# Loading the first tile of a masked softmax as two transfers instead of one

## The chip, the core and the metric

The kernel runs on one core of one Trainium2 chip. The metric is the device time of one execution in microseconds (us); the figure for a kernel is the median of several runs.

## What is computed

For each of 16 batch entries, a softmax over the last axis is taken over the first `length` columns only; the columns behind are zero in the output. The input is 16 x 8 x 256 x 256 float32, and the lengths lie between 128 and 255.

```python
result = np.zeros_like(x)
for b in range(batch):
    length = lengths[b]
    masked = x[b, :, :, :length].copy()
    masked = masked - np.max(masked, axis=-1, keepdims=True)
    exp_masked = np.exp(masked)
    result[b, :, :, :length] = exp_masked / np.sum(exp_masked, axis=-1, keepdims=True)
```

## The kernel before

One batch entry is one tile: 2048 rows of 256 numbers, laid out as 128 partitions x 16 rows x 256 columns, so that one partition holds 16 KB that are contiguous in memory. A tile is 2048 KB. Eight slots of the buffer `xt` hold tiles; a tile is loaded into its slot, worked on in place, and stored from there.

For each tile the engines do the following.

- VectorE (DVE) masks the upper half of the columns (`clip`, line 246): beyond the length the value becomes a very large negative number. For the first tile this is two instructions of eight rows each, for the others one of sixteen.
- ScalarE (ACT) takes the exponential in place: the first four rows in one instruction (line 372), the other twelve one by one with their row sums (line 375).
- DVE sums the first four rows (line 267), then for each half tile takes the reciprocal of the row sums (line 277) and multiplies (line 280).
- SyncE (SP) stores the tile in one to four pieces (line 152), each after the multiplication that it needs. SP also lets a tile's store wait until the stores of the tile two before have landed (line 151).

The loads come from two queues. SP issues the load of the first tile as its first transfer (line 143), and afterwards only stores: the hardware queue, called q1 in the profile, carries this load and all stores. GpSimd (POOL) issues the other fifteen loads on the software queue, q0. Three of them are issued at the start (line 194), after the mask limits are ready and one memset has run; the other twelve follow in a loop (line 166), each after an earlier load has landed and the slot's store is done. For most tiles only the columns up to a rounded length are loaded.

The first tile's load counts up the semaphore `s_ld[0]`, and DVE waits for its full count in `mask(0, ...)` before the first `clip`. A transfer's full count is 16. From there on DVE works through its instructions in a fixed order, and everything that it does later stands behind that first wait. SP's first store, two rows per partition of tile 0, waits for the first multiplication.

After the last tile DVE tests whether the sums were in range, and the program ends when the last store has landed.

Of the kernel before, what the change touches and what calls it, by code (L numbers as in the profile page):

```python
# [21 lines left out]
def kernel(  # L22
# [6 lines left out]
    nc = tc.nc  # L29
# [5 lines left out]
    nt = rows // P  # L35
# [4 lines left out]
    x_f = x.rearrange("b h q k -> b (h q) k").rearrange("b (p t) k -> b p t k", p=P)  # L40
# [9 lines left out]
    def batch_of(pos):  # L50
        return pos + 1 if pos < ahead - 1 else {ahead - 1: 15, 15: 0}.get(pos, pos)
# [22 lines left out]
    xt = pool.tile([P, slots, nt, seq_k], F32, name="xt")  # L74
# [24 lines left out]
    sem = lambda n: ctx.enter_context(nc.semaphore(n))  # L99
# [6 lines left out]
    with tc.tile_critical(sync_engine=POOL, no_gpsimd_drain=True):  # L106
# [1 line left out]
        s_ones = sem("s_ones")  # L108
        s_lenb = sem("s_lenb")
        s_lenf = sem("s_lenf")  # L110
        s_ld = [sem(f"s_ld{k}") for k in range(2)]

        s_sw = [sem("s_sw0"), sem("s_sw1")]

# [25 lines left out]


        nc.scalar.dma_start(out=word64, in_=lengths[None, :]).then_inc(s_word, 16)
        nc.sync.dma_start(out=xt[:, 0], in_=x_f[batch_of(0)]).then_inc(s_ld[0], 16)
        for b in range(batch):
            s_b = s_st[b % 2] if b < late else s_late if b < batch - 1 else s_last
            for s in parts(b):
# [3 lines left out]
                if 2 <= b < late and s.start == 0:  # L150
                    nc.sync.wait_ge(s_b, 64 * (b // 2 + 2))
                nc.sync.dma_start(
                    out=out_f[batch_of(b), :, s, :], in_=xt[:, b % slots, s, :]
# [67 lines left out]
        def step(ins):  # L221
# [8 lines left out]
                out=down, in0=iota_i, scalar1=0.5, scalar2=-big, op0=ALU.add, op1=ALU.mult  # L230
# [7 lines left out]
                out=len_s, in0=len_f, scalar1=big, scalar2=None, op0=ALU.mult  # L238
# [4 lines left out]
        def clip(b, s, lo, hi):  # L243

            t = xt[:, b % slots, s, lo:hi]
            return nc.vector.scalar_tensor_tensor(  # L246
                out=t,
                in0=down[:, None, lo:hi].to_broadcast([P, s.stop - s.start, hi - lo]),
                scalar=len_s[:, batch_of(b) : batch_of(b) + 1],
                in1=t,  # L250
                op0=ALU.add,
                op1=ALU.min,
            )

        def mask(b, s):
            if b == 0:
                nc.vector.wait_ge(s_ld[0], 16)
            elif b == ahead - 1:
                nc.vector.wait_ge(s_ld[1], 16)
            else:  # L260
                par = (b - 1 if b < ahead else b) % 2
                nc.vector.wait_ge(s_sw[par], 16 * max(b // 2, 1))
            clip(b, s, mid, seq_k).then_inc(s_min, 1)
# [10 lines left out]
        def divide(b, h):  # L274
# [10 lines left out]
            ).then_inc(s_out, 1)  # L285

        mask(0, slice(0, half))
        mask(0, slice(half, nt))
        total(0)
        for b in range(batch):  # L290


            first = b != 1
            if first:
                divide(b, 0)
            if b + 1 < batch:
                mask(b + 1, slice(0, nt))
            if not first:
                divide(b, 0)
            divide(b, 1)  # L300
            if b + 1 < batch:
                total(b + 1)
# [14 lines left out]
        for k, (_, _, edge, op) in enumerate(checks):  # L317
            nc.vector.tensor_scalar(  # L318
                out=bad[:, k : k + 1],
# [13 lines left out]
        with nc.vector.Else():  # L333
            with nc.Fori(0, batch, 1, engines=[DVE]) as i:
                nc.vector.wait_ge(g_ld, 16 * i + 16)
                nc.vector.scalar_tensor_tensor(
                    out=g_t,
# [8 lines left out]
                    out=neg_max, in_=g_t, op=ALU.max, axis=AX, negate=True  # L346
# [5 lines left out]
                    out=g_t,  # L352
# [10 lines left out]
        with nc.Fori(0, batch // slots, 1, engines=[ACT]) as turn:  # L363
            for slot in range(slots):
                for h in range(2):
# [7 lines left out]
                    for j in range(h * half + lump * (1 - h), (h + 1) * half):  # L373
                        e = xt[:, slot, j, :]
                        ins = nc.scalar.activation(  # L375
                            out=e, in_=e, func=EXP, accum_out=row_sum[:, slot, j : j + 1]
# [5 lines left out]
        with nc.scalar.If(a_redo >= 1):  # L382
# [4 lines left out]
            with nc.Fori(0, batch, 1, engines=[ACT]) as i:  # L387
                nc.scalar.dma_start(out=g_t, in_=x_g[:, bass.ds(i, 1)]).then_inc(g_ld, 16)
                nc.scalar.wait_ge(g_v, 3 * i + 2)
                with nc.Fori(0, nt, 1, engines=[ACT]) as t:  # L390
                    e = g_t[:, bass.ds(t, 1), :]
                    nc.scalar.activation(
                        out=e,
                        in_=e,
# [42 lines left out]
```

## Time and profile before

| | |
|---|---|
| median of 3 runs | 154.32 us (154.25 to 154.43) |
| the profiled execution | 154.43 us |
| its span in the trace | 152.8 us |
| DVE busy | 134.7 us |
| ACT busy | 95.0 us |
| bytes moved by the DMA engines | 61.57 MB, mean 403 GB/s |

The span begins with the first instruction in the trace and ends with the last event; what lies between span and time is outside the trace. A row of the timeline gives start and duration in us, the engine (SPq and POOLq are the queues from which SP and POOL issue), the line of the kernel, the operation, and in brackets the idle time before it and what ended it. A row of the windows gives one stretch of the span: busy time of each engine, and at the end the mean busy share of the 16 DMA engines and the rate in GB/s. A transfer over 128 partitions is spread over the 16 DMA engines, and a packet in the trace is one contiguous piece of it. A packet is counted in the stretch in which it starts, so a share can stand above 1.

### The profile page before, as it was taken

To read this page: it belongs to the slowest core of one execution; us is meant where nothing else is said; L and a number is where in the kernel's file an instruction comes from. 1 tells how busy PE (TensorE), PEld (TensorE's weight loads), DVE (VectorE), ACT (ScalarE), POOL (GpSimd) and SP (SyncE) were. 2 spreads that over 40 slices of the span, in tenths; PEclk is the share of its full clock that TensorE was granted. 3 is DMA by queue.
4 is the path that set the end of the run, shared out by engine and by line. 5 is a ranking of instruction groups with operands and counts; after the bars stand their busy time and mean duration, and the time that the engine had idled before them with its cause. 6 is when DMAs were issued, how large, how long until landed. Compare 5 with 4: busy or idle time off the path is not lost.

```text
span 152.8 us, 817 instructions
## 1 busy us (share of the span) xinstructions
PE 0.3 (0%) x2; PEld 0.2 (0%) x2; DVE 134.7 (88%) x107; ACT 95.0 (62%) x402; POOL 21.3 (14%) x29
## 2 busy tenths in 40 slices
PE   0000000000000000000000000000000000000000
PEld 0000000000000000000000000000000000000000
DVE  1058999999999999999999999999999999889920
ACT  3019599808668493939486684939394866829200
POOL 4961110030303020030300303011030000000000
DMA  4999999999999999999999999999999999999993
GB/s 107 425 425 433 422 413 389 444 412 408 406 396 421 402 421 414 415 408 402 428 411 420 415 414 413 418 414 414 419 419 420 416 419 417 425 442 429 431 418 154
DMA packets 10070, 61.57 MB, mean 403 GB/s; under 512 B 834, under 2 KB 946, under 8 KB 6226
## 3 DMA queue, kind: packets, MB, share of 16 engines
q1 hardware_dynamic: 5328, 35.65, 56.7%
q0 software_dynamic: 4736, 25.89, 41.7%
q14 instruction: 4, 0.03, 0.1%
q10 hardware_dynamic: 2, 0.00, 0.0%
HBM read 27.98 MB, written 33.55 MB: 403 GB/s over the span
## 4 chain that ended last, share of the span: by engine, by line
DMA 82%; DVE 8%; issue 3%; POOL 1%; POOLq 1%; PE 0%; ACTq 0%
DMA xt<-in_x_dram 82%; DVE xt L280 5%; DVE xt L246 2%; POOL xt L189 1%; DMA word<-in_lengths_dram 1%; DVE row_sum L267 1%; POOLq L166 1%; DVE ends L315 0%; POOL xt L194 0%; DVE inv_sum L277 0%; DVE bad L318 0%; DVE len_s L237 0%; PE len_f L214 0%; PE count L216 0%; DVE len_b L234 0%
## 5 line engine op out<-in xcount | busy, mean ns | idle before, releaser
L375 ACT ACTIVATE xt<-xt 128x256 f32<-128x256 f32 x192 | 76.6, 400 | 0.0
L280 DVE TENSOR_TENSOR xt<-xt,inv_sum 128x2048 f32<-128x2048 f32 x32 | 73.4, 2292 | 1.1
L372 ACT ACTIVATE xt<-xt 128x1024 f32<-128x1024 f32 x16 | 16.9, 1057 | 45.7 <-DVE xt L246 45.7
L246 DVE SCALAR_TENSOR_TENSOR xt<-down,len_s,xt 128x2048 f32<-128x2048 f32 (+1 forms) x17 | 37.7, 2220 | 7.2 <-DMA xt<-in_x_dram 7.2
L375 ACT ACTIVATION_READ_ACCUMULATOR xt<-xt 128x1 f32 x192 | 35.9, 187 | 0.0
L166 POOL DMA_DIRECT2D xt<-in_x_dram x12 | 13.3, 1106 | 90.5 <-DMA xt<-in_x_dram 72.8
L267 DVE TENSOR_REDUCE row_sum<-xt 128x4 f32<-128x1024 f32 x16 | 19.4, 1212 | 0.0
L277 DVE RECIPROCAL inv_sum<-row_sum 128x8 f32<-128x8 f32 x32 | 6.4, 199 | 0.9 <-ACT xt L375 0.4
L189 POOL MEMSET xt<- 128x1536 f32 x4 | 5.4, 1398 | 1.1 <-DVE len_s L237 1.1
L359 ACT ACT_TABLE_LOAD x1 | 1.3, 1283 | 1.6 <-PEq L421 1.6
L194 POOL DMA_DIRECT2D xt<-in_x_dram x3 | 1.8, 591 | 0.0
L229 DVE TENSOR_SCALAR down<-iota_i 128x256 f32<-128x256 int32 x1 | 0.3, 301 | 1.6 <-POOL iota_i L179 1.6
L315 DVE TENSOR_REDUCE ends<-inv_sum 128x1 f32<-128x256 f32 x2 | 0.7, 408 | 0.0
L237 DVE TENSOR_SCALAR len_s<-len_f 128x16 f32<-128x16 f32 x1 | 0.2, 174 | 0.4 <-PE len_f L214 0.4
L216 PE MATMUL count<-bad,ones_c 128*1 128x3 bf16 x1 | 0.2, 165 | 143.4 <-DVE bad L318 143.4
L234 DVE CAST len_b<-word 1x16 bf16<-1x16 int32 x1 | 0.2, 163 | 0.4 <-DMA word<-in_lengths_dram 0.4
L179 POOL IOTA iota_i<- 128x256 int32 x1 | 0.3, 333 | 0.6 <-POOLq L106 0.6
L326 DVE TENSOR_REDUCE redo<-count 1x1 f32<-1x3 f32 x1 | 0.1, 150 | 0.3 <-PE count L216 0.3
L318 DVE TENSOR_SCALAR bad<-ends 128x1 bf16<-128x1 f32 x3 | 0.3, 150 | 0.0
L185 POOL MEMSET seed<- 1x1 f32 x2 | 0.2, 226 | 0.0
L216 PEld LDWEIGHTS count<-bad,ones_c 128*1 128x1 bf16 x1 | 0.1, 79 | 143.5 <-DVE bad L318 143.5
L359 ACT ACTIVATE warm<-const-float32-0.0 128x1 f32<-128x1 f32 x1 | 0.2, 203 | 0.0
(10 smaller groups left out, 1.1 us busy)
## 6 DMA issues: line engine op xcount, KB each, us to landing
out_dram<-xt SPq DMA_DIRECT2D x23, 1024.0 KB
xt<-in_x_dram POOLq DMA_DIRECT2D x4, 2048.0 KB, 16.5
xt<-in_x_dram POOLq DMA_DIRECT2D x3, 1728.0 KB, 18.2
out_dram<-xt SPq DMA_DIRECT2D x9, 512.0 KB
out_dram<-xt SPq DMA_DIRECT2D x2, 2048.0 KB
xt<-in_x_dram POOLq DMA_DIRECT2D x2, 1600.0 KB, 17.7
xt<-in_x_dram POOLq DMA_DIRECT2D x2, 1280.0 KB, 17.7
xt<-in_x_dram SPq DMA_DIRECT2D x1, 2048.0 KB, 8.2
```

The costliest lines, as they stand in the source:

```text
L166: nc.gpsimd.dma_start(out=xt[:, slot, :, :w], in_=x_n[:, b, :, :w]).then_inc(s_sw[par], 16)
L189: nc.gpsimd.memset(xt[:, b, :, low:], 0.0).then_inc(s_fill, 1)
L194: nc.gpsimd.dma_start(out=xt[:, b], in_=x_f[batch_of(b)]).then_inc(s_sw[b - 1] if b < 3 else s_ld[1], 16)
L216: nc.tensor.matmul(count, lhsT=ones_c, rhs=bad, start=True, stop=True).then_inc(s_count, 1)
L246: return nc.vector.scalar_tensor_tensor(out=t, in0=down[:, None, lo:hi].to_broadcast([P, s.stop - s.start, hi - lo]), scalar=len_s[:, batc ...
L267: nc.vector.tensor_reduce(out=row_sum[:, b % slots, :lump], in_=xt[:, b % slots, :lump, :], op=ALU.add, axis=AX,).then_inc(s_exp[0], 1)
L277: step(nc.vector.reciprocal(out=inv_sum[:, b, s], in_=row_sum[:, b % slots, s]))
L280: nc.vector.tensor_tensor(out=t, in0=t, in1=inv_sum[:, b, s, None].to_broadcast([P, half, seq_k]), op=ALU.mult,).then_inc(s_out, 1)
L315: step(nc.vector.tensor_reduce(out=ends[:, k : k + 1], in_=values, op=op, axis=AX))
L359: nc.scalar.activation(out=warm, in_=nc.const_aps.tensor(0.0, (P, 1), F32), func=EXP)
L372: nc.scalar.activation(out=e, in_=e, func=EXP).then_inc(s_lump, 1)
L375: ins = nc.scalar.activation(out=e, in_=e, func=EXP, accum_out=row_sum[:, slot, j : j + 1])
```

## The change

The first tile is loaded by two transfers from SP, one behind the other on the same queue: rows 0 and 1 of each partition (2 KB per partition, 256 KB in all), then rows 2 to 15 (14 KB per partition, 1792 KB). Each has a semaphore of its own, `s_ld[0]` and the new `s_ld[2]`. Both calls of `mask` for the first tile wait for both semaphores, so no instruction of DVE uses the first two rows before the other fourteen are there. Nothing else differs; the order of the instructions on the other engines is the same.

```diff
-        s_ld = [sem(f"s_ld{k}") for k in range(2)]
+        s_ld = [sem(f"s_ld{k}") for k in range(3)]
...
-        nc.sync.dma_start(out=xt[:, 0], in_=x_f[batch_of(0)]).then_inc(s_ld[0], 16)
+        for k, s in enumerate((slice(0, 2), slice(2, nt))):
+            nc.sync.dma_start(out=xt[:, 0, s], in_=x_f[batch_of(0), :, s]).then_inc(
+                s_ld[2 * k], 16
+            )
...
             if b == 0:
-                nc.vector.wait_ge(s_ld[0], 16)
+                for k in (0, 2):
+                    nc.vector.wait_ge(s_ld[k], 16)
```

## The prediction

> **What bounds the kernel now.** I read the page first: busy times, the slices of the span, the DMA queues and the chain that ended last.
>
> ```profile
> span 152.8 us, 817 instructions
> PE 0.3 (0%) x2; PEld 0.2 (0%) x2; DVE 134.7 (88%) x107; ACT 95.0 (62%) x402; POOL 21.3 (14%) x29
> DMA  4999999999999999999999999999999999999993
> ...
> q1 hardware_dynamic: 5328, 35.65, 56.7%
> q0 software_dynamic: 4736, 25.89, 41.7%
> ...
> DMA 82%; DVE 8%; issue 3%; POOL 1%; POOLq 1%; PE 0%; ACTq 0%
> ```
>
> Two resources are nearly full. The DMA engines show 9 in every slice but the first and the last, and their two queues together fill 56.7 + 41.7 = 98.4% of the span. DVE is busy for 88%. The chain names DMA for 82%. Which of them sets the end must be read at the two ends of the span, because the change lies at the very start. First the timeline, at the start and near the end:
>
> ```profile
> 1.08 0.39 SPq L143 DMA_DIRECT2D xt<-in_x_dram  x1
> 4.36 1.76 POOL L194 DMA_DIRECT2D xt<-in_x_dram  x3
> 9.39 2.48 DVE L246 SCALAR_TENSOR_TENSOR xt<-down,len_s,xt 128x1024 f32<-128x1024 f32 x2 [6.40 <-DMA xt<-in_x_dram]
> 15.84 2.35 DVE L246 SCALAR_TENSOR_TENSOR xt<-down,len_s,xt 128x2048 f32<-128x2048 f32 x1
> 15.95 0.35 SPq L152 DMA_DIRECT2D out_dram<-xt  x1
> ...
> 134.12 2.35 DVE L246 SCALAR_TENSOR_TENSOR xt<-down,len_s,xt 128x2048 f32<-128x2048 f32 x1 [0.81 <-DMA xt<-in_x_dram]
> ...
> 142.75 2.29 DVE L280 TENSOR_TENSOR xt<-xt,inv_sum 128x2048 f32<-128x2048 f32 x1
> ```
>
> The list of waits has no other wait of DVE for a load:
>
> ```profile
> DVE xt L246 <- DMA xt<-in_x_dram: 7.2, 2, 6.4
> ```
>
> DVE waits for tile 0 until 9.39 and then runs without a wait for a load until just before 134.12, where it waits 0.81 us for the last tile to be masked. Its last multiplication starts at 142.75 and ends at 145.04. What the DMA engines have left by then stands in the windows of the last stages:
>
> ```profile
> 144.00:148.00 4.00, 0.17 (x1) 0.08 (x1) 2.20 (x8) 0.00 (x0) 0.00 (x0) 1.00 0.98 414
> 148.00:152.00 4.00, 0.00 (x0) 0.00 (x0) 0.00 (x0) 0.00 (x0) 0.00 (x0) 1.00 0.60 254
> ```
>
> After 145.04 they still move about 2.96 us x 414 GB/s + 4 us x 254 GB/s = 1225 + 1016 = 2241 KB. DVE's last half tile is 1049 KB of that (128 x 2048 x 4 bytes). So 1192 KB of older stores lie ahead of it, 2.9 us at 414 GB/s. The end is therefore set by the DMA engines working off their bytes. DVE could finish its last multiplication up to 2.9 us later before the DMA engines ran dry, and the first 0.81 us of a delay at the start would even be swallowed by the wait at 134.12. That is the main reading: **the time is the start of the first packets, plus all bytes at the DMA engines' rate, plus a tail**, and DVE's own start has slack.
>
> **The change part by part.** The rate of the packets comes from the DMA view, cut to the stretch from 5 to 6 us (tile 0's load alone), then 8 to 9 us (its last completion markers beside POOL's loads), then 20 to 21 us (POOL's loads beside SP's first store, which has 2 KB per partition).
>
> ```profile
> q1 hardware_dynamic: 25, 0.41, 96.2%
> ...
> q0 software_dynamic: 26, 0.43, 99.3%
> q1 hardware_dynamic: 12, 0.02, 4.4%
> ...
> q0 software_dynamic: 20, 0.33, 77.3%
> q1 hardware_dynamic: 21, 0.04, 11.0%
> ```
>
> A 16 KB packet takes 0.962 x 16 engine-us / 25 = 0.616 us. A 2 KB packet takes 0.110 x 16 / 21 = 0.084 us, against an eighth of the large one, 0.077. (The 2 KB packets are stores, the nearest row there is for 2 KB reads.) In the second stretch q1 has one data packet (0.02 MB) and eleven markers: 0.044 x 16 = 0.70 us, less 0.616, leaves 0.008 us per marker.
>
> 1. *Packets.* Before, each of the 16 DMA engines moves 8 packets of 16 KB and one marker: 4.94 us. After, it moves 8 of 2 KB, a marker, 8 of 14 KB (0.539 each) and a marker: 0.67 + 4.31 + 0.02 = 5.00. That is +0.06 us on the path that sets the end. Bounds: 0, if small reads go at the large ones' rate, and +0.13, twice that.
>
> 2. *SP.* One more issue of 0.39 us (row L143). SP's next transfer is the store at 15.95, so SP has over 13 us of cover and this costs nothing itself. What matters is whether the second transfer's packets reach the DMA engines before the first one's run out. They follow by 0.39 us in issue, and the first 256 KB last 0.67 us. If the trip from issue to engine is the same for both, there is no gap: 0.
>
> 3. *The start of the engines.* This is the term that the trace doesn't show for a split load, so it needs bounds. The windows of the first stretches:
>
> ```profile
> 2.00:2.50 0.50, 0.00 (x0) 0.00 (x0) 0.16 (x1) 0.50 (x1) 0.00 (x0) 1.00 1.84 328
> 2.50:3.00 0.50, 0.17 (x1) 0.10 (x1) 0.17 (x1) 0.49 (x2) 0.00 (x0) 1.00 0.18 33
> 3.00:3.50 0.50, 0.00 (x0) 0.00 (x0) 0.00 (x0) 0.14 (x1) 0.46 (x1) 1.00 0.95 262
> 3.50:4.00 0.50, 0.00 (x0) 0.00 (x0) 0.00 (x0) 0.00 (x0) 0.50 (x1) 1.00 0.86 360
> 4.00:4.50 0.50, 0.00 (x0) 0.00 (x0) 0.00 (x0) 0.00 (x0) 0.50 (x2) 1.00 0.93 393
> ```
>
> From 2.0 to 2.5 us ten packets start (328 GB/s x 0.5 us = 164 KB), and they take 1.84 x 0.5 x 16 / 10 = 1.47 us each, more than twice the 0.616 of later ones. One more starts before 3.0, and the others of the 16 engines only after that. From 2.0 to 4.0 the engines start (328 + 33 + 262 + 360) x 0.5 = 492 KB; at the steady 393 they would start 786 KB. So the start-up loses 294 KB, or 0.75 us. With smaller first packets that loss can shrink to nothing (-0.75) or come a second time for the second transfer (+0.75). I take 0: the late engines and the slow first packets look like a wait until data begins to flow, at about 3 us, and the same bytes then flow whichever way they are cut. The nearest row for packets of 2 KB, 0.084 us, shows no cost of a fresh start.
>
> 4. *DVE.* Two waits more, already met when reached. The 32 multiplications of line 280 each stand behind a wait, and idle 1.1 us in all:
>
> ```profile
> L280 DVE TENSOR_TENSOR xt<-xt,inv_sum 128x2048 f32<-128x2048 f32 x32 | 73.4, 2292 | 1.1
> ```
>
> That is 0.034 us each, so 0 to 0.07 us for two, on DVE and under its cover. If the 2.9 us were gone, they would be paid in full.
>
> 5. *Landing of tile 0.* DVE's start moves with the later of the two markers. Terms 1 and 3 put it at +0.06, with ends at -0.75 and +0.8. There is one further effect. POOL's first three loads, issued at 4.36, have their first packets after 7 us (the DMA view from 6 to 7 us, where q1 is alone, and from 7 to 8 us):
>
> ```profile
> q1 hardware_dynamic: 29, 0.48, 111.3%
> ...
> q1 hardware_dynamic: 24, 0.31, 72.9%
> q0 software_dynamic: 5, 0.08, 19.1%
> ```
>
> Tile 0's packets thus go ahead of POOL's in nearly all cases. With 14 KB packets, each engine has more of them outstanding when POOL's arrive. If one POOL packet gets in between, that engine's marker comes 0.62 us later; if two, 1.23. DVE would then start at 10.0 to 10.6 instead of 9.39, POOL's packets just that much earlier. No DMA engine idles for it. SP's stores begin later, but until about 20 us the engines have POOL's loads to do: three tiles of 2097 KB at 414 GB/s alone are 15.2 us from about 8. At the other end DVE's cover is 2.9 us. So this costs nothing; without the cover it would cost 0.6 to 1.2.
>
> Sum: +0.06 (packets) + 0 (SP) + 0 (start-up) + 0 (DVE) + 0 (landing). The profiled run was 154.43 with a span of 152.8, so 1.6 us lie outside the trace and stay. It becomes 154.49; the median of the runs stands 0.11 below the profiled one, and 154.32 + 0.06 gives **154.4 us**. A measurement of this kernel can tell about 0.2%, 0.31 us, from no change, so this is "the same".
>
> **The rivals.**
>
> *A second start-up (slower).* On the engines that start late, the second transfer's packets come after the first's are done, and the start-up loss of 0.75 us is paid again, with all 16 engines idle or slow and no other load in the queue: POOL issues at 4.36 and its packets start after 7. Time: 154.32 + 0.06 + 0.75 = 155.1. For it: the first ten engines start nearly 1 us before the last five, so handing out a transfer seems to take longer than the 0.39 us of its issue, and the second must wait for the first. Against it: the late engines also run their small packets late. It decides from the point where an engine gets its second batch more than 0.67 us after its first. Chance 0.28.
>
> *The two transfers one after the other (slower).* If the second moved only once the first had landed, the trip itself would be paid twice. The load landed 8.2 us after its issue, of which 4.94 are packets, so the trip and the start-up are 3.3.
>
> ```profile
> xt<-in_x_dram SPq DMA_DIRECT2D x1, 2048.0 KB, 8.2
> ```
>
> POOL's packets could fill the engines in the last part, from about 6 us; about 2 us of idle would remain, 156.4. Against it: SP waits for nothing between the two. The Trainium skill's page "DMA: Bandwidth & Descriptors" (Anatomy of one DMA) gives a software-queue DMA a fixed 2.0 us besides its bytes, and its rules for authors want at least 1 MiB per transfer; by that the 256 KB piece would add 2.0 us, if it were paid in sequence. No run here shows two loads in a row on an empty queue. Chance 0.04.
>
> *A shorter start-up (faster).* If the slow first packets are slow because each engine must finish 16 KB before going on, 2 KB pieces get through sooner. Half of the 0.75 us would be won on the engines' path: 154.32 + 0.06 - 0.38 = 154.0; a gain beyond 0.75 is excluded, as no more is lost. Against it: after 4 us the same 16 KB packets run at full rate, so size alone isn't slow. Chance 0.21.
>
> *The split has no use at all.* DVE waits for both parts, so nothing starts earlier on two rows; that is within my forecast.
>
> **How the numbers follow.** My forecast (154.1 to 154.6) has 0.47, the second start-up 0.28, the serial trip 0.04, the shorter start-up 0.21. The range of 153.9 to 155.1 takes in the forecast, most of the faster case and the second start-up up to its full price; it leaves out the serial trip and the far ends, about 0.15. Faster by over 0.2%: 0.21; within: 0.47; slower: 0.32.
>
> **What would show it.** In the profile after: two L144 issues on SP, 0.39 us apart; in the windows from 2.0 to 4.0 us about 492 KB started again (clearly more speaks for the shorter start-up, clearly less for the second); `clip` of tile 0 between 9.2 and 10.6; the wait before the last mask shrinking by whatever DVE starts later; DMA share still near 1 up to 150 us. I am wrong if the end moves with DVE's start although stores are still queued behind its last multiplication, or if the DMA engines idle in the middle of the span.

## The result, and the profile after

The changed kernel takes 154.75 us (median of 22 runs, 154.46 to 156.03), against 154.37 us for the kernel before (22 runs beside it, 154.18 to 154.77). The ratio is 1.0031, with a 95% interval of 1.0020 to 1.0043: slower by about 0.5 us (the two medians lie 0.38 us apart), a little more than the 0.2% that the prediction took as the bound of "the same". In two further measurements it was 1.0031 (1.0019 to 1.0043) and 1.0027 (1.0017 to 1.0037). The profiled execution took 154.76 us, its span is 153.1 us. The runs also scatter more: 1.6 us from the lowest to the highest, against 0.6.

First the timeline after, then its waits:

```profile
1.08 0.86 SPq L144 DMA_DIRECT2D xt<-in_x_dram  x2
4.37 1.76 POOL L197 DMA_DIRECT2D xt<-in_x_dram  x3
9.64 2.48 DVE L249 SCALAR_TENSOR_TENSOR xt<-down,len_s,xt 128x1024 f32<-128x1024 f32 x2 [6.64 <-DMA xt<-in_x_dram]
16.20 0.34 SPq L155 DMA_DIRECT2D out_dram<-xt  x1
...
134.02 2.35 DVE L249 SCALAR_TENSOR_TENSOR xt<-down,len_s,xt 128x2048 f32<-128x2048 f32 x1 [0.47 <-DMA xt<-in_x_dram]
142.64 2.29 DVE L284 TENSOR_TENSOR xt<-xt,inv_sum 128x2048 f32<-128x2048 f32 x1
```

```profile
DVE xt L249 <- DMA xt<-in_x_dram: 7.1, 2, 6.6
```

The first mask starts 0.25 us later (9.64 for 9.39). In this execution the delay isn't seen at the end: the wait for the last tile is 0.47 instead of 0.81, and the last multiplication starts at 142.64, even 0.11 earlier. Yet the span is 0.3 us longer. DVE did not lengthen it.

The DMA engines ran behind. The windows give the rate in the last column; here first the kernel before, then the changed one:

```profile
2.00:4.00 2.00, 0.17 (x1) 0.10 (x1) 0.34 (x2) 1.13 (x2) 0.96 (x1) 1.00 0.96 246
4.00:6.00 2.00, 0.00 (x0) 0.00 (x0) 0.00 (x0) 0.00 (x0) 2.00 (x4) 1.00 0.94 401
6.00:10.00 4.00, 0.00 (x0) 0.00 (x0) 0.61 (x1) 0.00 (x0) 4.00 (x4) 1.00 1.02 434
50.00:144.00 94.00, 0.00 (x0) 0.00 (x0) 92.02 (x68) 64.31 (x275) 8.07 (x7) 1.00 1.02 418
144.00:152.00 8.00, 0.17 (x1) 0.08 (x1) 2.20 (x8) 0.00 (x0) 0.00 (x0) 1.00 0.79 334
```

```profile
2.00:4.00 2.00, 0.17 (x1) 0.10 (x1) 0.34 (x2) 1.12 (x2) 0.95 (x1) 1.00 0.94 267
4.00:6.00 2.00, 0.00 (x0) 0.00 (x0) 0.00 (x0) 0.00 (x0) 2.00 (x4) 1.00 0.93 387
6.00:10.00 4.00, 0.00 (x0) 0.00 (x0) 0.36 (x1) 0.00 (x0) 4.00 (x4) 1.00 0.99 414
50.00:144.00 94.00, 0.00 (x0) 0.00 (x0) 92.36 (x68) 64.29 (x275) 8.04 (x7) 1.00 1.02 418
144.00:152.00 8.00, 0.17 (x1) 0.08 (x1) 2.09 (x8) 0.00 (x0) 0.00 (x0) 1.00 0.81 344
```

Rate times length gives the KB started in each stretch. By 10 us the kernel before has started 492 + 802 + 1736 = 3030 KB, the changed one 534 + 774 + 1656 = 2964: it leads by 42 KB at 4 us and is 66 KB behind at 10. From 50 to 144 us both run at 418 GB/s; over 94 us one GB/s is 94 KB, so this row alone can't tell whether the changed kernel catches up. The last row can: after 144 us 2672 KB are left before (8 x 334), 2752 after. These 80 KB more are, at 418 GB/s, 0.19 us of the 0.33 between the two profiled executions. Packets are counted where they start, so such a figure is uncertain by some tens of KB; the second profile of the kernel before, below, differs by 32.

### The profile page after: what moved, and what is told of

Read it like the earlier page. It is cut to its first block, busy times and chain, and to the rows that moved or that the text cites. A ratio compares the mean times of both kernels' runs of the same rounds, so it can differ in the third digit from the quotient of the medians.

```text
span 153.1 us, 819 instructions
## 1 busy us (share of the span) xinstructions
PE 0.3 (0%) x2; PEld 0.2 (0%) x2; DVE 134.7 (88%) x107; ACT 95.0 (62%) x402; POOL 21.3 (14%) x29
## 3 DMA queue, kind: packets, MB, share of 16 engines
q1 hardware_dynamic: 5472, 35.65, 56.5%
## 4 chain that ended last, share of the span: by engine, by line
DMA 82%; DVE 8%; issue 3%; POOL 1%; POOLq 1%; PE 0%; ACTq 0%
DMA xt<-in_x_dram 81%; DVE xt L284 4%; DVE xt L249 2%; POOL xt L192 1%; DMA word<-in_lengths_dram 1%; DVE row_sum L271 1%; POOLq L169 1%; DVE ends L319 0%; POOL xt L197 0%; DVE inv_sum L281 0%; DVE bad L322 0%; DVE len_s L240 0%; PE len_f L217 0%; PE count L219 0%; DVE len_b L237 0%
```

## The experiments

Each ratio is to the kernel before, run beside it on the same chip.

**What the ratios are worth.** The kernel before as an experiment of its own, unchanged:

> The kernel before once more, as any other kernel: every theory expects a ratio of 1.000. How far it lies from 1 shows what the other ratios are worth, and a second profile shows how far the first 10 us and the stretch from 20 to 28 us scatter by themselves.

Measured: 154.27 us, ratio 1.0000 (0.9991 to 1.0009). Its second profile:

```profile
2.00:4.00 2.00, 0.17 (x1) 0.10 (x1) 0.34 (x2) 1.12 (x2) 0.95 (x1) 1.00 1.03 254
4.00:6.00 2.00, 0.00 (x0) 0.00 (x0) 0.00 (x0) 0.00 (x0) 2.00 (x4) 1.00 0.94 401
6.00:10.00 4.00, 0.00 (x0) 0.00 (x0) 0.60 (x1) 0.00 (x0) 4.00 (x4) 1.00 1.02 438
144.00:152.00 8.00, 0.17 (x1) 0.08 (x1) 1.61 (x8) 0.00 (x0) 0.00 (x0) 1.00 0.78 330
```

By 10 us 508 + 802 + 1752 = 3062 KB, 32 ahead of its first profile, and 2640 left after 144 us, 32 fewer. So a lead at 10 us can be seen again at the end, but both profiled executions took 154.43 us: 32 KB don't show in the time. Nor does the end of DVE's work: here its last multiplication starts 0.59 us earlier than in the first profile (142.16 for 142.75). And the wait for the last tile is 0.21 instead of 0.81 without any change, so a wait some tenths shorter, as in the changed kernel, doesn't by itself show a delay that was swallowed.

```profile
133.53 2.35 DVE L246 SCALAR_TENSOR_TENSOR xt<-down,len_s,xt 128x2048 f32<-128x2048 f32 x1 [0.21 <-DMA xt<-in_x_dram]
...
142.16 2.29 DVE L280 TENSOR_TENSOR xt<-xt,inv_sum 128x2048 f32<-128x2048 f32 x1
```

**The changed kernel twice more**, no edit:

> The changed kernel once more. Theory A (a second start-up: the first large packets after the small ones are slow again, so all DMA engines run some 0.1 to 0.5 us behind, for good): ratio 1.0025 (+0.4 us), the DMA engines behind the kernel before from about 9 us on. Theory B (DVE's later start sets the end): the same ratio, but the DMA engines level with the kernel before until DVE's start, about 9.6 us, and the loss later. Theory C (the two kernels differ only by scatter): ratio within 0.001 of 1.

> The changed kernel a third time: ratio 1.003. If the loss is a start-up of varying length, the rate from 2 to 4 us lies between those of its first two profiles (267 and 135 GB/s) or near one of them, and the time goes with the KB that are missing by 10 us.

Measured: 154.82 us, 1.0031 (1.0019 to 1.0043), and 154.67 us, 1.0027 (1.0017 to 1.0037). Their profiled executions took 155.07 and 154.72 us. The windows of the second profile, then of the third:

```profile
2.00:4.00 2.00, 0.17 (x1) 0.10 (x1) 0.34 (x2) 1.12 (x2) 0.95 (x1) 1.00 0.97 135
4.00:6.00 2.00, 0.00 (x0) 0.00 (x0) 0.00 (x0) 0.00 (x0) 2.00 (x4) 1.00 0.95 397
6.00:10.00 4.00, 0.00 (x0) 0.00 (x0) 0.00 (x0) 0.00 (x0) 4.00 (x4) 1.00 1.02 434
144.00:152.00 8.00, 0.17 (x1) 0.08 (x1) 2.71 (x8) 0.00 (x0) 0.00 (x0) 1.00 0.84 354
```

```profile
2.00:4.00 2.00, 0.17 (x1) 0.10 (x1) 0.34 (x2) 1.12 (x2) 0.95 (x1) 1.00 0.99 246
4.00:6.00 2.00, 0.00 (x0) 0.00 (x0) 0.00 (x0) 0.00 (x0) 2.00 (x4) 1.00 0.89 373
6.00:10.00 4.00, 0.00 (x0) 0.00 (x0) 0.06 (x1) 0.00 (x0) 4.00 (x4) 1.00 0.98 416
144.00:152.00 8.00, 0.17 (x1) 0.08 (x1) 2.12 (x8) 0.00 (x0) 0.00 (x0) 1.00 0.82 348
```

By 10 us they are 230 and 128 KB behind the first profile of the kernel before, and after 144 us 160 and 112 KB more are left than there. With the first profile of the change that makes three executions:

| | behind by 10 us | left over after 144 us | the same at 418 GB/s | longer than the first profiled execution before |
|---|---|---|---|---|
| first | 66 KB | 80 KB | 0.19 us | 0.33 us |
| second | 230 KB | 160 KB | 0.38 us | 0.64 us |
| third | 128 KB | 112 KB | 0.27 us | 0.29 us |

Each is behind by 10 us, and by how much differs from one execution to the next. That fits the wider scatter of this kernel's runs. The deficit at 10 us and the one at the end have the same sign, not the same size, and the time doesn't simply go with the KB missing by 10 us, as was expected of the third: 62 KB more are missing there than in the first, and it took 0.04 us less. The rest of the time, 0.02 to 0.26 us, isn't resolved by these counts. Nor is the stretch in which the KB go missing always the same: from 2 to 4, 4 to 6 and 6 to 10 us the first execution gains 42, loses 28 and loses 80 KB, the second loses 222, 8 and 0, the third 0, 56 and 72.

Which packets are slow is seen in the DMA view from 2 to 3 us and from 3 to 4 us, here of the first, the second and the third profile:

```profile
q1 hardware_dynamic: 112, 0.22, 65.1%
...
q1 hardware_dynamic: 51, 0.32, 123.2%
```

```profile
q1 hardware_dynamic: 93, 0.19, 151.1%
...
q1 hardware_dynamic: 24, 0.08, 43.8%
```

```profile
q1 hardware_dynamic: 98, 0.19, 78.3%
...
q1 hardware_dynamic: 60, 0.30, 120.0%
```

In the second profile the 93 packets of 2 KB that start from 2 to 3 us take 1.511 x 16 / 93 = 0.26 us on average, though the same size took 0.084 later. From 3 to 4 us only 24 start. So here the small packets themselves stand still on the engines, and the large ones behind them start late.

In the other two it is mainly the large packets behind them. In the first profile, from 2 to 3 us, a packet takes 0.651 x 16 / 112 = 0.09 us, about the price in full flow, and in the third 0.783 x 16 / 98 = 0.13. But of the 51 packets that start from 3 to 4 us in the first profile, the bytes allow only about 19 of 14 KB beside the rest of the small ones and the markers, and these 19 must take about 0.9 us each to fill 1.232 x 16 us, where the prediction reckoned 0.539. The third gives about 0.9 us for some 16 large ones. The kernel before is slow once too, with its first 16 KB packets at 1.47 us. So each execution has slow packets at about 3 us: the small ones in one of these three, the second transfer's first large ones in the other two.

**The order turned round.** `(slice(0, nt - 2), slice(nt - 2, nt))` for `(slice(0, 2), slice(2, nt))`, nothing else:

> Still two transfers, but the 14 rows first and the 2 rows behind them: the same packets, markers and semaphores, in the other order. Theory A: the large packets pay the start-up once and the small ones come in full flow, so the loss goes: ratio 1.000 to 1.001. Theory of cost per packet and marker: as the change, 1.003. Theory B: ratio follows the first mask's start; if that lies 0.25 us late again, 1.003.

Measured: 154.37 us, 1.0003 (0.9994 to 1.0013).

```profile
2.00:4.00 2.00, 0.17 (x1) 0.10 (x1) 0.34 (x2) 1.12 (x2) 0.94 (x1) 1.00 0.92 258
4.00:6.00 2.00, 0.00 (x0) 0.00 (x0) 0.00 (x0) 0.00 (x0) 2.00 (x4) 1.00 0.96 394
6.00:10.00 4.00, 0.00 (x0) 0.00 (x0) 1.08 (x1) 0.00 (x0) 4.00 (x4) 1.00 1.03 428
144.00:152.00 8.00, 0.17 (x1) 0.08 (x1) 1.86 (x8) 0.00 (x0) 0.00 (x0) 1.00 0.78 332
```

Its first mask:

```profile
8.92 2.48 DVE L249 SCALAR_TENSOR_TENSOR xt<-down,len_s,xt 128x1024 f32<-128x1024 f32 x2 [5.92 <-DMA xt<-in_x_dram]
```

The same packets, markers, issues and waits, and the loss is gone: 3016 KB by 10 us, 2656 left after 144. This excludes a cost per transfer, per packet or per marker as the main cause of this change's loss. It is the 2 KB packets standing first that costs. The first mask, too, starts 0.72 us earlier than in the first profile of the change; whether that matters is tried below, where DVE's start is moved alone.

**More and other pieces.** Four transfers of four rows, each with a semaphore of its own, and DVE waits for all four:

```diff
...
-        for k, s in enumerate((slice(0, 2), slice(2, nt))):
+        for k in range(4):
+            s = slice(4 * k, 4 * k + 4)
...
```

> Tile 0 as four transfers of four rows (4 KB packets), DVE waits for all. Theory A in the form of a cost per transfer: three additional transfers instead of one, ratio about 1.008 (+1.2 us). Theory A in the form of a cost of small followed by large packets: no such step here, ratio about 1.000 to 1.001. Cost per packet and marker: 24 packets and 3 markers more per engine instead of 8 and 1, ratio about 1.009.

Two transfers of eight rows, `(slice(0, half), slice(half, nt))`:

> Two transfers of eight rows each (8 KB packets), DVE waits for both. Theory A as a cost per transfer: as the change, 1.003. Theory A as a cost of small first packets: between the changed kernel (2 KB) and the 14 KB first packets, about 1.001.

Measured: four parts 155.39 us, 1.0061 (1.0048 to 1.0075); halves 154.44 us, 1.0014 (1.0003 to 1.0026). With first packets of 2, 8, 14 and 16 KB the ratios are 1.0031, 1.0014, 1.0003 and 1, but this is no scale. The four parts, with 4 KB, lose most, and the two kernels with waits of their own, below, give 1.0003 with 8 KB first and 1.0012 with 14. From 8 KB up nothing is told apart. The 2 KB kernel lies above these in each of its three measurements, though its intervals touch that of the halves. The four parts were expected at 1.000 to 1.001 by "small followed by large" and refute that form, since their packets are all alike. Both other forms expected too much, 1.008 and 1.009. Two of their windows:

```profile
2.00:4.00 2.00, 0.17 (x1) 0.10 (x1) 0.34 (x2) 1.12 (x2) 0.95 (x1) 1.00 0.84 201
4.00:6.00 2.00, 0.00 (x0) 0.00 (x0) 0.00 (x0) 0.00 (x0) 2.00 (x4) 1.00 0.99 369
```

and their DMA view from 6 to 7 us, when POOL has issued its loads, and from 7 to 8 us:

```profile
q1 hardware_dynamic: 97, 0.36, 106.7%
...
q1 hardware_dynamic: 107, 0.39, 96.0%
```

The 0.36 MB are about 88 packets of 4 KB, the others markers, so one takes 1.067 x 16 / 88 = 0.19 us from 6 to 7 us, and from 7 to 8 us, reckoned in the same way, 0.16. Four of them take 0.78 and 0.65, while 16 KB in one packet took 1.113 x 16 / 29 = 0.614 in the same stretch of the kernel before (row in the prediction). So 4 KB packets lose at the start (90 of the 210 KB that they are behind by 10 us are missing by 4) and go on losing after it. After 144 us 192 KB more are left than in the kernel before, 0.46 us of the 1.00 between the profiled executions; their first mask starts at 11.10, and the rest isn't accounted for. What POOL's issue has to do with the slow packets from 6 to 7 us was not tried.

The halves' own profile doesn't fit a loss at the start: 266, 414 and 438 GB/s in the three windows, 82 KB ahead by 10 us. Their rate from 20 to 50 us is 406 GB/s against 410, and their profiled execution took 154.50 us. After 144 us they have 16 KB more left than the kernel before, so a lead at 10 us can be lost on the way; why, stays open.

**DVE's start, later and earlier.** One transfer as before, and two operations on a scratch tile between the wait for tile 0 and the first mask:

```diff
+    junk = pool.tile([P, 2, seq_k], F32, name="junk")
...
                 nc.vector.wait_ge(s_ld[0], 16)
+                if s.start == 0:
+                    for k in range(2):
+                        nc.vector.tensor_scalar(
+                            out=junk[:, k], in0=iota_i, scalar1=0.5, scalar2=-big,
+                            op0=ALU.add, op1=ALU.mult,
+                        )
```

> One transfer as before; two operations of 0.3 us on a scratch tile stand on DVE between the wait for tile 0 and its first mask, so DVE starts about 0.55 us later, twice the 0.25 us of the changed kernel. Theory A (DVE's start has cover, as predicted): ratio within 0.001 of 1, the wait before the last mask shorter by about 0.5 us. Theory B (DVE's start sets the end): +0.55 us, ratio 1.0035.

Eight and eight rows, each mask waiting for its own half:

```diff
-                for k in (0, 2):
-                    nc.vector.wait_ge(s_ld[k], 16)
+                nc.vector.wait_ge(s_ld[2 * (s.start // half)], 16)
```

> Two transfers of eight rows, and the first mask waits for the first transfer alone, the second mask for the second. DVE starts about 2 us earlier on its first half. If the time goes with DVE's start on this side too (the late start of 0.97 us cost 0.0015), the ratio is 0.997 to 0.999; if DVE's start has cover and the DMA engines set the end, it is that of the halves without this, 1.0014, or 1.000.

The same wait with fourteen rows first:

> Fourteen rows first, then two; the first mask waits for the fourteen rows alone. DVE starts about 0.6 us earlier than with one transfer. If the DMA engines set the end: ratio 1.000 to 1.0005, as the same order without this. If DVE's start counts: 0.999.

Measured: late 154.49 us, 1.0015 (1.0006 to 1.0024); halves with their own waits 154.34 us, 1.0003 (0.9994 to 1.0012); fourteen rows first with its own wait 154.48 us, 1.0012 (1.0003 to 1.0021). The first masks, in this order:

```profile
10.41 2.47 DVE L247 SCALAR_TENSOR_TENSOR xt<-down,len_s,xt 128x1024 f32<-128x1024 f32 x2
```

```profile
6.32 1.28 DVE L249 SCALAR_TENSOR_TENSOR xt<-down,len_s,xt 128x1024 f32<-128x1024 f32 x1 [3.34 <-DMA xt<-in_x_dram]
```

```profile
8.31 2.48 DVE L249 SCALAR_TENSOR_TENSOR xt<-down,len_s,xt 128x1024 f32<-128x1024 f32 x2 [5.32 <-DMA xt<-in_x_dram]
```

DVE's start 3.07 us earlier (6.32 for 9.39) wins nothing, and 1.08 us earlier wins nothing either. So DVE's start doesn't set the end from that side. The late start is 1.02 us late, not the 0.55 expected: the two operations took 0.97 us, and tile 0 landed a little later. It costs 0.15%, about 0.2 us (0.1 to 0.4 by the interval), where its cover should have made it free. Its transfers are those of the kernel before, and by 10 us it has started 32 KB more than the first profile of that (3062). So a late start of DVE costs something by itself: about a fifth of the delay comes through. None of these versions is faster than the kernel before.

**The slow stretch moved.** SP waits for the mask limits, `nc.sync.wait_ge(s_v, 2)`, ahead of the one load, and ahead of the two loads:

> The single transfer, but SP waits for the mask limits (about 3.0 us) before it issues, so its packets start about 2 us later. If the slow stretch at the start belongs to the first load (cold), it moves along: slow from 4 to 6 us, ratio about 1.012 (+2 us less what POOL's loads fill in). If it belongs to the clock time of 2 to 4 us (something else that runs then), the load comes in at full rate and the ratio is about 1.007.

> The two transfers of the change behind the same wait. Theory A (small packets first make the start-up slower): against the late single transfer another +0.002 to +0.004 in the ratio. If the slow stretch belongs to 2 to 4 us, the split costs nothing here: the same ratio as the late single transfer within 0.001.

Measured: 156.45 us, 1.0136 (1.0121 to 1.0151), and 156.67 us, 1.0150 (1.0135 to 1.0165). From 4 to 6 us, one load and then the split:

```profile
4.00:6.00 2.00, 0.00 (x0) 0.00 (x0) 0.00 (x0) 0.00 (x0) 2.00 (x4) 1.00 1.03 254
```

```profile
4.00:6.00 2.00, 0.00 (x0) 0.00 (x0) 0.00 (x0) 0.00 (x0) 2.00 (x4) 1.00 0.87 177
```

The first 2 us of the late load run at 254 GB/s, as the first 2 us of the early one did at 246. So the slow stretch belongs to the first load, not to something else that runs from 2 to 4 us. The split starts 154 KB less in it, and is 130 KB behind by 10 us. But this loss doesn't reach the end: after 144 us it has 24 KB more left, the profiled executions took 156.74 and 156.73 us, and in both the first mask starts at 13.66. The ratios differ by 0.0014, between the two expectations, and their intervals overlap. With DVE 4.27 us late in both, DVE may set the end here, which would hide the DMA engines' loss; that was not shown.

**Two queues.** Rows 0 and 1 from SP, the other fourteen from ACT:

```diff
-        for k, s in enumerate((slice(0, 2), slice(2, nt))):
...
+        nc.scalar.dma_start(out=xt[:, 0, 2:], in_=x_f[batch_of(0), :, 2:]).then_inc(s_ld[2], 16)
+        nc.sync.dma_start(out=xt[:, 0, 0:2], in_=x_f[batch_of(0), :, 0:2]).then_inc(s_ld[0], 16)
```

> The two transfers on two queues: rows 0 and 1 from SP, the other fourteen from ACT, behind its transfer of the lengths. If the loss comes from the second transfer standing behind the first in one queue, it goes: ratio 1.000 to 1.001. If it comes from small packets during the start-up, on whatever queue, part of it stays: about 1.002.

Measured: 155.55 us, 1.0066 (1.0044 to 1.0087). It is slower than either theory expected, and doesn't decide between them. The ACT transfer lands 10.5 us after its issue, so the first mask starts at 12.27, and that alone may cost some tenths:

```profile
xt<-in_x_dram ACTq DMA_DIRECT2D x1, 1792.0 KB, 10.5
```

## Why the prediction was right or wrong

The time, 154.75 us, lies in the range of 153.9 to 155.1, but above the forecast's own band of 154.1 to 154.6. What happened is nearer to the first rival, a second start-up, at about half of its price (+0.4 to +0.5 us for +0.81). The range held because it took in that rival, not because the sum was right.

*The main reading* held: the DMA engines' bytes set the end: all three profiles of the change have fewer bytes started by 10 us and more left after 144, the kernel before takes the same time with DVE's last multiplication 0.59 us earlier, and a DVE start 3 us earlier is worth nothing. It held for small shifts: the late pair shows a case in which 130 KB less by 10 us cost nothing measurable.

*Term 1 (packets, +0.06) and term 2 (SP, 0)* held as far as the runs tell: with the order turned round, all these are paid, and the ratio is 1.0003, or 1.0012 with the wait of its own. The second issue cost 0.47 us on SP instead of 0.39 (0.86 for two) and nobody waited for it.

*Term 3 (the start of the engines, taken as 0, bounds -0.75 to +0.75)* is the step that failed. By 10 us 66, 230 and 128 KB were missing, 0.16, 0.55 and 0.31 us at 418 GB/s. The sign that the prediction named was too short for this: from 2 to 4 us the three profiles start 534, 270 and 492 KB, so that by it one speaks for the shorter start-up, one for the second, and one for the forecast. A packet counts where it starts, and slow packets that start before 4 us cost bytes only after that. I argued that the same bytes would flow whichever way they are cut, and took a row of 2 KB packets from 20 us, in full flow, as the nearest for packets at the start. The runs show that during the start-up a 2 KB packet can take 0.26 us on average for 0.084, or, where the small ones pass in time, the first 14 KB packets behind them about 0.9 for 0.539.

*The rival of a second start-up* had the right sign, and in part the right mechanism: in the first and the third profile the second transfer's first packets are slow after the small ones were not, as it said. But it is no cost of a second transfer as such, for two transfers in the other order lose nothing, and in the worst profile it is the first transfer's small packets that stand still. Why small packets prolong the start-up was not found.

*Term 4 (DVE's waits)* can't be told apart at 0.07 us. *Term 5 (landing, 0)*: the first mask started at 9.64, 10.81 and 9.94 in the three profiles, the middle one beyond my 10.6. The rows of the second and third:

```profile
10.81 2.48 DVE L249 SCALAR_TENSOR_TENSOR xt<-down,len_s,xt 128x1024 f32<-128x1024 f32 x2 [7.82 <-DMA xt<-in_x_dram]
```

```profile
9.94 2.48 DVE L249 SCALAR_TENSOR_TENSOR xt<-down,len_s,xt 128x1024 f32<-128x1024 f32 x2 [6.96 <-DMA xt<-in_x_dram]
```

The cover was good but not full: at 0.2 us per 1.02 us of delay, delays of 0.25, 1.42 and 0.55 are worth 0.05, 0.28 and 0.11 us, an estimate from one late kernel. So part of the 0.5 us may come through DVE's late start, part from the DMA engines' own delay; the runs don't divide them.

*The serial trip* is out. In the first profile the two transfers landed 3.0 and 8.0 us after their issues, which lie less than 0.5 us apart; SP waited for nothing in between. The fixed 2.0 us that the Trainium skill's page "DMA: Bandwidth & Descriptors" (Anatomy of one DMA) gives a software-queue transfer did not appear as 2.0 us of time on this hardware queue: the second transfer cost about 0.5 us in one order and nothing measurable in the other. No run here tries it on the software queue. *The shorter start-up* was there for 2 us only, and in one profile: the change leads by 42 KB at 4 us in its first and has lost the lead by 10.

## What to carry to other kernels

Where the DMA engines are busy from the first packet to the last, compare two kernels by the KB started up to a time: it shows on which side of a stage a loss lies. Check it at the end too, for here a deficit of 66 to 230 KB at the start came back with the same sign, but a lead of 82 KB and a deficit of 130 KB did not. A first transfer that is cut needs a reason, such as work that starts on the first piece; of the two orders tried here, the large piece first was the cheaper. And a price for a packet in full flow is no price for one in the start-up. One profile can show an extreme: in the worst of three the small packets stood still, in the other two mainly the large ones behind them.

## What the runs showed of the hardware that was not expected

The first 2 us of the first load are slow in both places tried: 246 GB/s from 2 us, against 401 in the 2 us that follow, and 254 GB/s when the load is issued 2 us later. With 2 KB first, two executions started far less in this stretch (135 GB/s, and 177 in the late pair) and two did not (267 and 246). Two transfers on one hardware queue in the order large, small cost nothing measurable (1.0003), although the page of the profile then counts 144 packets more on the queue (5472 against 5328, as in the change).
